# Two token mixers of an encoder trunk on one Trainium2 core: weight remainders moved from GpSimd to VectorE, output sums merged, and the order of TensorE's work around the scan groups and the attention rows changed

## The chip, the core and the metric

The kernel runs on one core of one Trainium2 chip. A core has TensorE (matmuls into PSUM banks), VectorE, ScalarE, GpSimd and SyncE, the last of which here only issues DMAs. The profile calls them PE (with PEld for TensorE's loads of stationary operands), DVE, ACT, POOL and SP. The metric is the time of one execution in microseconds on the device.

## The reference

512 tokens of width 1024 in float32 go through two layers. Each layer adds a mixer and a gated FFN to the residual stream:

```python
def even_mixer(x, ...):                        # layer 0
    proj = rms_norm(x, mix_norm) @ w_in        # q, k, v | z, xbc, dt
    na_out = neighbourhood_attention(q, k, v, na_rel_bias)      # 8 heads of 64
    xbc = silu(centred_depthwise_conv(xbc, conv_w, conv_b))     # xs, bm, cm
    y = ssd_scan(forward) + flip(ssd_scan(backward)) + D_skip * xs   # 16 heads, 4 groups, chunks of 128
    ssd_out = gated_group_rms_norm(y, z, out_norm)              # norm over a group's 256 columns
    return concatenate([na_out, ssd_out]) @ w_out
def odd_mixer(x, ...):                         # layer 1
    q, k, v = split(rms_norm(x, mix_norm) @ w_qkv)              # 16 query heads, 4 key/value heads of 64
    q, k = apply_rope(rms_norm(q)), apply_rope(rms_norm(k))
    return softmax(q @ k.T * scale) @ v @ w_out
def swiglu_ffn(x, norm_g, w13, w2):            # after each mixer
    g, u = split(rms_norm(x, norm_g) @ w13)
    return (silu(g) * u) @ w2
```

## The kernel before

Activations lie with the channels on the 128 partitions and the 512 tokens along the free axis. The residual stream is eight tiles of 128x512, `res[0..7]`. A float32 product is made of three matmuls: each operand is split into a high half (a rounded copy, made by ScalarE, names ending in `h`) and a low half (the remainder, one subtraction, names ending in `l`), and `mm3` adds low by high, high by low and high by high in one PSUM bank. The `w_l`, `wq_l`, `wo_l` of the profile are such remainders of weights, made in `load_w`: SyncE loads a raw block, ScalarE copies it, and the engine given as `eng` subtracts.

TensorE's filler work is a generator. `stream(blocks, ahead)` goes through weight blocks and yields after each `mm3` (three matmuls, called a step here), and `run(n)` does n steps. What lies between the steps is the work with dependent chains.

`even_mixer` records TensorE's order by hand in its second half (the other engines' order is found by the Tile scheduler). There are four scan groups g. The projections of group g are steps 64+48g to 64+48(g+1); the last step of its fourth channel block triggers one Silu over 128x3072 (L545). `LEAD[g]` steps later, `ssd_group` begins with the transposes `bt` (L563), `xt` and the products `cb`, then, with `SSD_QUOTA[g]` steps between its phases, the states `st`, the first `yd`/`yo` (L651, L664) and the second. `NORM_LAG[g]` steps after the group's end come the row sums `gs` (L688) for its normalisation, whose results `so_xh`, `so_xl` are operands of the output products. Those products are the last filler: `oA` for each of 8 output tiles, over 8 of the 10 operand blocks, and after every three tiles a "rest" with the two blocks of the third group (weights `wq{0,3,6}`). The last group's two blocks are done at the end, in `tail`.

`odd_mixer` is ordered by the Tile scheduler on all engines. Filler work is the q projections of query groups 1 to 3 and then the output products (`out_blocks`), whose operands `ctxb` come out of the attention. In iteration i, `scores(i)` makes two score tiles `os`, maximum (L1276, VectorE), exponential (ScalarE), reciprocal, and a rescaling on GpSimd (L1280); transposes follow two and values three iterations later. `quota[i]` steps of filler are spread over iteration i. A finished q projection triggers the rotation and norm of the group (`q_finish`), whose remainders `qa_sl`, `qb_sl` are made on GpSimd, like `cx_sl` of finished heads. The remainders of the value weights (`wgvl`, L1349) and of all filler weights (`wq_l`, `wo_l`) are also GpSimd's. The output products come in three parts of two operand blocks, each part once over all 8 output tiles with one addition to `res` for each tile (L1328); the fourth part is in `tail`.

In the FFNs the order of TensorE, VectorE and ScalarE is written out. The last lines add each of the final products to `res` and store it (L994, L996).

## Time and profile before

| | |
|---|---|
| time, median of 3 runs | 1282.05 us (1279.4 to 1282.43) |
| profiled execution, its own time | 1281.94 us |
| its span, first to last instruction | 1280.2 us |
| TensorE busy | 1258.6 us, 98% of the span |
| VectorE, ScalarE, GpSimd busy | 990.8, 723.9, 154.4 us |
| mean granted TensorE clock | 0.996 of full speed |

The span lacks what lies before the first and after the last instruction, 1.74 us here. A busy engine has an instruction running; TensorE's matmuls overlap, so 128x512 matmuls that last 0.39 us each follow one another every 0.227 us. The granted clock is given as a share of full speed.

### The profile page before, as it was taken

The page shows a single profiled execution, that of the slowest core. Times are in us where ns is not written, and L with a number is a line of the kernel's source. Part 1 is how long each engine was busy: PE and PEld are TensorE (multiplying, and loading weights), DVE is VectorE, ACT ScalarE, POOL GpSimd, SP SyncE. Part 2 cuts the span into 40 slices and gives each one's busy share as a digit, 9 for nine tenths or more (in the row PEclk, how much of TensorE's full clock was granted, in tenths as well). Part 3 has the DMA queues.
Part 4 walks back from the last instruction along what each step waited for, and adds up shares of the span by engine and source line. Part 5 has one row for each costly group of instructions (what it writes and reads, how often), then busy time and mean ns, then how long its engine had stood idle before and what let it go on. Part 6 is the DMA issues. An engine that isn't in the chain of part 4 may idle for free.

```text
span 1280.2 us, 19995 instructions
## 1 busy us (share of the span) xinstructions
PE 1258.6 (98%) x7502; PEld 1100.6 (86%) x7502; DVE 990.8 (77%) x1649; ACT 723.9 (57%) x1367; POOL 154.4 (12%) x177
## 2 busy tenths in 40 slices
PE   9999999999999999999999999999999999999998
PEld 8778788777888899989998878778888999889987
DVE  6788798898689888739953778998889988549732
ACT  6676578778365455515633548867564556325521
POOL 5022111011000000000000325655100000000000
PEclk9999999999999999999999999999999999999999
DMA  6335443546332333323223352321223333323132
GB/s 232 103 108 158 111 141 116 165 128 193 108 132 83 107 108 114 118 82 100 77 79 109 132 116 83 83 67 34 86 80 99 115 102 114 115 82 100 55 118 93
DMA packets 52081, 139.03 MB, mean 109 GB/s; under 512 B 6992, under 2 KB 8144, under 8 KB 51984
## 3 DMA queue, kind: packets, MB, share of 16 engines
q1 hardware_dynamic: 51696, 137.23, 35.0%
q8 instruction: 59, 0.97, 0.3%
q10 hardware_dynamic: 288, 0.52, 0.1%
q14 instruction: 38, 0.31, 0.1%
HBM read 127.11 MB, written 2.23 MB: 101 GB/s over the span
## 4 chain that ended last, share of the span: by engine, by line
PE 71%; DVE 14%; ACT 7%; issue 4%; DMA 2%; POOL 0%; SPq 0%; DVEq 0%; ACTq 0%; POOLq 0%
PE fo L160 5%; PE fo L161 5%; PE fo L162 5%; PE fa L162 5%; PE fa L161 5%; PE fa L160 5%; PE fb L162 3%; PE fb L161 3%; PE fb L160 3%; PE opt L1289 2%; PE g L160 2%; PE g L161 2%; PE g L162 2%; PE vps L281 2%; PE fc L162 1%
## 5 line engine op out<-in xcount | busy, mean ns | idle before, releaser
L147 ACT ACTIVATE wf_h<-wf_r 128x1024 fp32r<-128x1024 f32 (+1 forms) x76 | 69.5, 919 | 125.9 <-PE fo L162 68.0
L160 PE MATMUL fo<-hh,wf_l 128*128 128x512 f32 x352 | 137.2, 390 | 0.4 <-DVE wf_l L149 0.4
L161 PE MATMUL fo<-hl,wf_h 128*128 128x512 f32 x352 | 137.0, 389 | 0.0
L162 PE MATMUL fo<-hh,wf_h 128*128 128x512 f32 x352 | 136.9, 389 | 0.0
L994 DVE TENSOR_TENSOR xr<-xr,fo 128x512 f32<-128x512 f32 x48 | 32.2, 685 | 111.3 <-PE fo L162 111.3
L149 DVE TENSOR_TENSOR wf_l<-wf_r,wf_h 128x1024 fp32r<-128x1024 f32 (+1 forms) x76 | 78.8, 1054 | 15.5 <-ACT wf_h L147 15.5
L160 PEld LDWEIGHTS fo<-hh,wf_l 128*128 128x128 f32 x352 | 66.1, 188 | 14.7 <-DVE wf_l L149 1.2
L162 PEld LDWEIGHTS fo<-hh,wf_h 128*128 128x128 f32 x352 | 66.1, 188 | 13.9
L161 PEld LDWEIGHTS fo<-hl,wf_h 128*128 128x128 f32 x352 | 66.1, 188 | 13.5
L160 PE MATMUL g<-n_xh,w_l 128*128 128x512 f32 x192 | 76.8, 400 | 0.0
L161 PE MATMUL g<-n_xl,w_h 128*128 128x512 f32 x192 | 75.1, 391 | 0.5 <-DVE n_xl L184 0.5
L162 PE MATMUL g<-n_xh,w_h 128*128 128x512 f32 x192 | 75.3, 392 | 0.0
L920 ACT ACTIVATE sl<-sb 128x256 f32<-128x256 f32 x34 | 14.2, 419 | 90.7 <-DVE sb L919 90.7
L1349 POOL TENSOR_TENSOR wgvl<-wgv_r,wgvh 128x512 fp32r<-128x512 f32 x4 | 6.5, 1635 | 402.2 <-ACT wgvh L1348 400.3
L1280 POOL TENSOR_SCALAR op<-op,osum 128x512 f32<-128x512 f32 x64 | 45.7, 723 | 54.0 <-DVE osum L1279 36.1
L1278 ACT ACTIVATE op<-os,omx 128x512 f32<-128x512 f32 x64 | 43.5, 685 | 13.6 <-DVE omx L1276 12.2
L1292 ACT ACTIVATE opt<-opt 128x512 fp32r<-128x512 f32 x64 | 38.1, 598 | 20.4 <-PE opt L1289 20.1
L1293 DVE TENSOR_TENSOR opt<-opt,opt 128x512 fp32r<-128x512 f32 x64 | 43.6, 684 | 5.6 <-ACT opt L1292 4.7
L801 ACT ACTIVATE sa<-fa 128x256 f32<-128x256 f32 x68 | 25.4, 374 | 36.9 <-PE fa L162 36.9
L1276 DVE TENSOR_REDUCE omx<-os 128x1 f32<-128x512 f32 x64 | 42.0, 681 | 5.2 <-PE os L1274 5.1
L801 ACT ACTIVATE gh<-gr 128x1024 fp32r<-128x1024 f32 x34 | 35.6, 1047 | 13.7 <-PE fo L162 8.8
L161 PEld LDWEIGHTS g<-n_xl,w_h 128*128 128x128 f32 x192 | 36.1, 188 | 7.4 <-DVE n_xl L184 0.8
(2635 smaller groups left out, 4354.0 us busy)
## 6 DMA issues: line engine op xcount, KB each, us to landing
ur<-in_w_fa SPq DMA_DIRECT2D x34, 512.0 KB, 3.5
gr<-in_w_fa SPq DMA_DIRECT2D x34, 512.0 KB, 3.6
w_r<-in_w_ssd SPq DMA_DIRECT2D x24, 512.0 KB, 3.6
wf_r<-in_w_fa SPq DMA_DIRECT2D x20, 512.0 KB, 3.6
wf_r<-in_w_fb SPq DMA_DIRECT2D x32, 320.0 KB, 3.0
wf_r<-in_w_fb SPq DMA_DIRECT2D x16, 512.0 KB, 3.6
wo_r<-in_w_o SPq DMA_DIRECT2D x14, 512.0 KB, 3.8
nb<-in_nab SPq DMA_DIRECT2D x16, 256.0 KB, 3.2
```

The lines of the kernel that those rows point to most:

```text
L147: A.activation(hi[:, 0:cols], raw, AF.Copy)
L149: (eng or V).tensor_tensor(lo[:, 0:cols], raw, f(hi)[:, 0:cols], ALU.subtract)
L160: T.matmul(ps, wl[:, a], xh[:, b], start=first, stop=False, skip_group_check=skip)
L161: T.matmul(ps, wh[:, a], xl[:, b], start=False, stop=False, skip_group_check=skip)
L162: T.matmul(ps, wh[:, a], xh[:, b], start=False, stop=last, skip_group_check=skip)
L801: A.activation(dst, src, AF.Copy, scale=scale)
L994: V.tensor_tensor(res[o], res[o], self.banks[o], ALU.add)
L1276: V.tensor_reduce(mx, sps, AX.X, ALU.max, negate=True)
L1278: A.activation(p_, sps, AF.Exp, bias=mx, accum_out=sums)
L1280: G.tensor_scalar(p_, p_, sums, 1.0, ALU.mult, ALU.mult)
L1292: A.activation(hl[:, 0:S], pt, AF.Copy)
L1293: V.tensor_tensor(hl[:, S:2 * S], pt, f(hl[:, 0:S]), ALU.subtract)
```

## The change

1. `vec`, the small table of gains, is loaded by ScalarE's DMA queue instead of SyncE's, ahead of everything.
2. In `even_mixer`, `LEAD`, `SSD_QUOTA` and `NORM_LAG` get other numbers. The largest: the last group begins 12 steps after its projections instead of 0, its row sums come 12 instead of 14 steps after it, the third group's row sums 10 instead of 6 steps after that group, and between the third group's two output halves no step is left.
3. In `odd_mixer`, 16 remainders of weights (six `wq_l` and six `wo_l` of 128x1024, four `wgvl` of 128x512) go from GpSimd to VectorE. The remainders of activations and the rescaling stay on GpSimd.
4. The output products of parts 0 and 1 are summed in one bank: 12 matmuls a bank, two output tiles from a weight block, one addition where there were two (8 additions fewer). They begin when both parts' operands are there. Part 2 stays as it was.
5. The quota of iterations 9, 14, 18, 21 and 25 becomes 8, 0, 5, 9 and 4, where it was 2, 2, 2, 3 and 2 (all others are equal or differ by one).
6. The last output tile of the second FFN is added and stored in two halves.

The number of matmuls is the same.

```diff
-LEAD = (12, 12, 12, 0)
-SSD_QUOTA = ((10, 8, 10, 2, 12), (10, 8, 10, 2, 12), (10, 8, 10, 2, 12), (10, 8, 10, 2, 12))
-NORM_LAG = (12, 12, 6, 14)
+OD_FILL = 8
+OD_AFTER = 4
+OD_QUOTA = (5, 5, 4, 2, 2, 2, 2, 2, 2, 8, 2, 2, 2, 2, 0, 2, 3, 2, 5, 2, 2, 9, 2, 2, 2, 4, 3, 2, 2, 3, 2, 2, 3, 3, 3)
+LEAD = (15, 12, 14, 12)
+SSD_QUOTA = ((10, 9, 10, 2, 12), (10, 8, 10, 2, 12), (10, 8, 10, 0, 12), (10, 8, 10, 2, 12))
+NORM_LAG = (12, 12, 10, 12)
...
+        nc.scalar.dma_start(vect, vec)
         A.preload_act_table_set(LNEXP)
...
-        nc.sync.dma_start(vect, vec)
...
                 if k == self.hi - 1:
-                    V.tensor_tensor(res[o], res[o], self.banks[o], ALU.add)
-                    if self.final and layer == 1:
-                        nc.sync.dma_start(out[o], res[o])
+                    last = self.final and layer == 1
+                    for at in (LOH, HIH) if last and o == KB - 1 else (ALL,):
+                        V.tensor_tensor(res[o][:, at], res[o][:, at], self.banks[o][:, at], ALU.add)
+                        if last:
+                            nc.sync.dma_start(out[o][:, at], res[o][:, at])
...
-        def out_blocks(part):
-            def matmuls(w, half):
-                while ctxb[2 * part + 1] is None:
+        def out_blocks(parts):
+            per = 8 // (2 * len(parts))
+
+            def matmuls(w, t):
+                while ctxb[2 * parts[-1] + 1] is None:
                     yield
-                for o in range(4 * half, 4 * half + 4):
-                    ps = bank(f"o1{part}_{o}")
-                    for k in range(2):
-                        mm3(ps, w, (o % 4 * 2 + k) * P, ctxb[2 * part + k], ALL, k == 0, k == 1)
-                        yield
+                for n in range(per):
+                    o = per * t + n
+                    ps = bank(f"o1{parts[0]}_{o}")
+                    for m, part in enumerate(parts):
+                        for k in range(2):
+                            mm3(ps, w, ((m * per + n) * 2 + k) * P, ctxb[2 * part + k], ALL, m + k == 0,
+                                k == 1 and part == parts[-1])
+                            yield
                     V.tensor_tensor(res[o], res[o], ps, ALU.add)
...
+            def load(t):
+                half, at = divmod(t * per, 4)
+                return load_w([w_o1[part, half][:, 2 * P * at:2 * P * (at + per)] for part in parts], 1024,
+                              f"wo{parts[0]}_{t}", V)
...
-            G.tensor_tensor(lo, part, f(hi), ALU.subtract)
+            V.tensor_tensor(lo, part, f(hi), ALU.subtract)
...
-        blocks = (list(q_blocks(1, G)) + list(q_blocks(2, G)) + list(q_blocks(3, G))
-                  + [b for part in range(3) for b in out_blocks(part)])
+        blocks = (list(q_blocks(1, V)) + list(q_blocks(2, V)) + list(q_blocks(3, V))
+                  + [b for parts in ((0, 1), (2,)) for b in out_blocks(parts)])
...
-            n = quota[i]
+            n = OD_QUOTA[i]
```

Three places in the order show what moves. The first is TensorE at the end of the third scan group (number 2: `yo` is its last product) and the start of the last one (`bt` reads `grp`, the Silu's result). Before:

```order
L664 MATMUL yo_1_0_2992<-grp_392,H_2698 128x128 x3
L664 MATMUL yo_1_1_3001<-grp_392,H_2698 128x128 x3
L563 MATMUL bt_3020<-cstt,grp_393 128x128 x4
L570 MATMUL xt_0_3027<-cstt,grp_393 128x128 x4
L570 MATMUL xt_1_3034<-cstt,grp_393 128x128 x4
L576 MATMUL cb_3041<-grp_393 128x128 x4
L160 MATMUL oA_2963<-so_0_xh,wo_l 128x512
```

Now:

```order
L667 MATMUL yo_1_0_2992<-grp_392,H_2704 128x128 x3
L667 MATMUL yo_1_1_3001<-grp_392,H_2704 128x128 x3
L163 MATMUL oA_2963<-so_0_xh,wo_l 128x512
L164 MATMUL oA_2963<-so_0_xl,wo_h 128x512
L165 MATMUL oA_2963<-so_0_xh,wo_h 128x512
...
L163 MATMUL oA_3032<-nch_1663,wo_l 128x512
L164 MATMUL oA_3032<-ncl_1664,wo_h 128x512
L165 MATMUL oA_3032<-nch_1663,wo_h 128x512
L566 MATMUL bt_3045<-cstt,grp_393 128x128 x4
L573 MATMUL xt_0_3052<-cstt,grp_393 128x128 x4
```

Eighteen `oA` matmuls of 512 columns stand between `yo` and `bt` where none stood. Behind them the third group's row sums `gs` come 36 `oA` and `st` matmuls ahead of the first "rest" (the first use of that group's normalised blocks), where they came 48 ahead; the 12 that are gone are `oA`.

The second place is VectorE in the second half of scan group 1. `cf` is an operand of TensorE's `yd` (L651), `grp` a convolution (L528), `w_5_l` the remainder of a weight block. Before:

```order
L646 TENSOR_TENSOR cf_2444<-cf_2444,m_2443 128x512
L644 TENSOR_TENSOR cf_2466<-cf_2466,cb_2467 128x512
L528 SCALAR_TENSOR_TENSOR grp_392<-g_3_2435,vect,grp_392 128x510
L149 TENSOR_TENSOR w_5_l<-w_5_r,w_5_h 128x1024
L646 TENSOR_TENSOR cf_2466<-cf_2466,m_2465 128x512
L528 SCALAR_TENSOR_TENSOR grp_392<-g_3_2435,vect,grp_392 128x511
L149 TENSOR_TENSOR w_0_l<-w_0_r,w_0_h 128x1024
```

Now:

```order
L649 TENSOR_TENSOR cf_2444<-cf_2444,m_2443 128x512
L531 SCALAR_TENSOR_TENSOR grp_392<-g_3_2435,vect,grp_392 128x510
L649 TENSOR_TENSOR cf_2466<-cf_2466,m_2465 128x512
L531 SCALAR_TENSOR_TENSOR grp_392<-g_3_2435,vect,grp_392 128x511
L152 TENSOR_TENSOR w_5_l<-w_5_r,w_5_h 128x1024
```

Both `cf` products come ahead of the remainder `w_5_l`.

The third place is VectorE in the attention of `odd_mixer` around iterations 9 and 10: `omx` and `osum` belong to score tiles, `q_ra`, `q_rb` and `oq_m` to the rotation and norm of a query group, `opt` to transposed probabilities. Before:

```order
L1276 TENSOR_REDUCE omx<-os_2_8313 128x1
L1276 TENSOR_REDUCE omx<-os_3_8323 128x1
L1315 TENSOR_TENSOR ocx_8301<-oc_8221,oct_8302 64x512
L1152 TENSOR_TENSOR q_rb_8337<-q_1_8055,qt_tab 128x512
L1293 TENSOR_TENSOR opt_1_8310<-opt_1_8305,opt_1_8310 128x512
L1279 RECIPROCAL osum<-osum 128x1
L1153 TENSOR_TENSOR q_ra_8336<-q_ra_8336,q_rb_8337 128x512
L1279 RECIPROCAL osum<-osum 128x1
L1151 TENSOR_TENSOR q_ra_8341<-q_0_7870,qt_tab 128x512
L1152 TENSOR_TENSOR q_rb_8342<-q_1_8055,qt_tab 128x512
L1195 SCALAR_TENSOR_TENSOR oq_m<-oq_ss,oem 128x512
L1153 TENSOR_TENSOR q_ra_8341<-q_ra_8341,q_rb_8342 128x512
```

Now:

```order
L1281 TENSOR_REDUCE omx<-os_2_8314 128x1
L152 TENSOR_TENSOR wq_1_l<-wq_1_r,wq_1_h 128x1024
L1284 RECIPROCAL osum<-osum 128x1
L1281 TENSOR_REDUCE omx<-os_3_8324 128x1
L152 TENSOR_TENSOR wo_0_l<-wo_0_r,wo_0_h 128x1024
L1284 RECIPROCAL osum<-osum 128x1
L1158 TENSOR_TENSOR q_ra_8337<-q_ra_8337,q_rb_8338 128x512
L1157 TENSOR_TENSOR q_rb_8343<-q_1_8055,qt_tab 128x512
L1200 SCALAR_TENSOR_TENSOR oq_m<-oq_ss,oem 128x512
L1158 TENSOR_TENSOR q_ra_8342<-q_ra_8342,q_rb_8343 128x512
L1298 TENSOR_TENSOR opt_0_8404<-opt_0_8399,opt_0_8404 128x512
L152 TENSOR_TENSOR wo_1_l<-wo_1_r,wo_1_h 128x1024
```

Three remainders of 128x1024 stand between the small operations; the rotation's first products have moved ahead of these rows. Between score tiles 13 and 22, two more such remainders come, and three additions to `res` (L1328) stand where six stood; two products of a rotation leave that stretch to earlier rows.

A fourth move needs no rows. On ScalarE, in front of the attention, the copy `wq1_1_h` stood between the logarithm and the exponential of the key norm `ok_r`; now it stands behind that norm's three operations. On VectorE the sum `oqsq`, which TensorE's first head-norm product waits for, now has `wq_1_l`, two of the four `wgvl` and both `kab` remainders ahead of it on that norm's chain, where only one `kab` was.

## Rows read from the trace of the kernel before

**Rows 1.** The page's busy engines, and its group of GpSimd's rescaling.

```profile
PE 1258.6 (98%) x7502; PEld 1100.6 (86%) x7502; DVE 990.8 (77%) x1649; ACT 723.9 (57%) x1367; POOL 154.4 (12%) x177
...
L1280 POOL TENSOR_SCALAR op<-op,osum 128x512 f32<-128x512 f32 x64 | 45.7, 723 | 54.0 <-DVE osum L1279 36.1
```

**Rows 2.** Waits of PE by line and releaser: us in total, times, longest.

```profile
PE os L1273 <- ACT op L1278: 2.7, 1, 2.7
PE oq_ss L1193 <- DVE oqsq L1243: 2.4, 1, 2.4
...
PE os L1273 <- DVE oq_m L1195: 1.4, 1, 1.4
```

**Rows 3.** Windows: length, busy PE, PEld, DVE, ACT, POOL; PEclk, DMA share, GB/s.

```profile
289.90:293.60 3.70, 3.63 (x21) 3.63 (x21) 1.87 (x5) 3.44 (x6) 0.00 (x0) 0.60 0.92 247
...
741.00:744.00 3.00, 3.00 (x12) 2.02 (x11) 3.00 (x4) 0.79 (x3) 2.36 (x1) 0.59 0.72 158
...
804.80:808.50 3.70, 3.67 (x24) 3.25 (x24) 3.70 (x7) 2.98 (x6) 0.00 (x0) 1.00 0.12 48
...
795.99:862.40 66.41, 61.44 (x352) 50.08 (x350) 60.46 (x113) 50.13 (x106) 40.23 (x38) 0.97 0.26 72
862.40:918.80 56.40, 56.40 (x342) 48.97 (x342) 49.11 (x96) 38.73 (x82) 23.56 (x27) 1.00 0.17 57
817.90:830.05 12.15, 11.23 (x73) 9.40 (x72) 10.16 (x21) 9.81 (x23) 7.34 (x11) 1.00 0.41 109
830.05:849.00 18.95, 16.50 (x95) 13.52 (x93) 18.81 (x32) 13.66 (x27) 11.65 (x10) 1.00 0.17 58
```

**Rows 4.** Timeline of the first microseconds: start, duration, engine, instruction, [idle before <-releaser].

```profile
0.73 0.39 SPq L240 DMA_DIRECT2D vect<-in_vec  x1
1.18 0.42 SPq L249 DMA_DIRECT2D x<-in_xt  x1
```

**Rows 5.** Timeline, end of scan group 2 to the third "oA" behind it.

```profile
287.15 2.76 ACT L545 ACTIVATE grp<-grp 128x3072 f32<-128x3072 f32 x1
...
289.97 1.11 PE L563 MATMUL bt<-cstt,grp 128*128 128x128 f32 x4 [3.96 <-ACT grp L545]
...
298.19 0.39 PE L160 MATMUL oA<-so_xh,wo_l 128*128 128x512 f32 x1
...
299.78 0.39 PE L161 MATMUL oA<-so_xl,wo_h 128*128 128x512 f32 x1
```

**Rows 6.** Timeline around the first "rest" of the output products.

```profile
307.82 0.74 DVE L184 SCALAR_TENSOR_TENSOR so_xl<-yn,vect,so_xh 128x512 fp32r<-128x512 f32 x1
...
309.95 0.39 PE L161 MATMUL oA<-so_xl,wq_h 128*128 128x512 f32 x1
```

**Rows 7.** Timeline in the second half of scan group 1.

```profile
237.53 1.21 DVE L149 TENSOR_TENSOR w_l<-w_r,w_h 128x1024 fp32r<-128x1024 f32 x1
...
239.40 1.09 PE L651 MATMUL yd<-cf,xtok 128*64 128x128 f32 x14 [0.83 <-DVE cf L646]
```

**Rows 8.** Timeline from the key norm to the first head-norm product of odd_mixer.

```profile
727.72 2.27 DVE L218 TENSOR_TENSOR ortt<-ort 128x4 f32<-128x4 f32 x1 [1.24 <-ACT ort L217]
730.02 0.16 DVE L203 SCALAR_TENSOR_TENSOR ortt<-ortt,ortm 128x4 f32<-128x4 f32 x1
...
732.34 1.04 ACT L147 ACTIVATE wq_h<-wq_r 128x1024 fp32r<-128x1024 f32 x1
...
734.60 1.81 DVE L203 SCALAR_TENSOR_TENSOR ok_t<-ok_t,ok_m 128x512 f32<-128x512 f32 x1 [2.10 <-ACT ok_t L211]
...
740.31 0.68 DVE L1204 TENSOR_TENSOR kab<-k_ra,kab 128x512 fp32r<-128x512 f32 x1
```

**Rows 9.** VectorE's groups from 756 to 919: busy, mean ns | idle before.

```profile
L1255 DVE TENSOR_TENSOR q_ra<-q_ra,oq_r 128x512 f32<-128x512 f32 x6 | 5.9, 1020 | 0.0
L1153 DVE TENSOR_TENSOR q_ra<-q_ra,q_rb 128x512 f32<-128x512 f32 x6 | 5.8, 963 | 0.0
...
L149 DVE TENSOR_TENSOR wt_l<-wt_r,wt_h 128x1024 fp32r<-128x1024 f32 x2 | 2.4, 1221 | 0.3 <-ACT wt_h L147 0.3
```

More of the change, by code (lines that the diff above doesn't have):

```diff
@@ L1243, in matmuls @@
                     V.tensor_tensor(sqs[0], sqs[0], sqs[1], ALU.add)
-                    after(4, lambda: q_finish(g, banks, sqs[0]))
+                    after(OD_AFTER, lambda: q_finish(g, banks, sqs[0]))
             sqs = []
@@ L1317, in values @@
                 ctxb[h // 2] = split(cx, f"cx{h}", xgslot if h >= 12 else ctxslot, V if h >= 14 else G)
-        def out_blocks(part):
-            def matmuls(w, half):
-                while ctxb[2 * part + 1] is None:
+        def out_blocks(parts):
+            per = 8 // (2 * len(parts))
+            def matmuls(w, t):
+                while ctxb[2 * parts[-1] + 1] is None:
                     yield
-                for o in range(4 * half, 4 * half + 4):
-                    ps = bank(f"o1{part}_{o}")
-                    for k in range(2):
-                        mm3(ps, w, (o % 4 * 2 + k) * P, ctxb[2 * part + k], ALL, k == 0, k == 1)
-                        yield
-                    V.tensor_tensor(res[o], res[o], ps, ALU.add)
-            for half in range(2):
-                yield (lambda half=half: load_w(w_o1[part, half], 1024, f"wo{part}_{half}", G)), \
-                    (lambda w, half=half: matmuls(w, half))
+                for n in range(per):
[6 more added lines that the diff above has]
+                            yield
+                    V.tensor_tensor(res[o], res[o], ps, ALU.add)
+            def load(t):
+                half, at = divmod(t * per, 4)
+                return load_w([w_o1[part, half][:, 2 * P * at:2 * P * (at + per)] for part in parts], 1024,
+                              f"wo{parts[0]}_{t}", V)
+            for t in range(8 // per):
+                yield (lambda t=t: load(t)), (lambda w, t=t: matmuls(w, t))
         def run(gen, n=None):
@@ L1369, in odd_mixer @@
             step(True)
-        blocks = (list(q_blocks(1, G)) + list(q_blocks(2, G)) + list(q_blocks(3, G))
-                  + [b for part in range(3) for b in out_blocks(part)])
+        blocks = (list(q_blocks(1, V)) + list(q_blocks(2, V)) + list(q_blocks(3, V))
+                  + [b for parts in ((0, 1), (2,)) for b in out_blocks(parts)])
         fill = stream(blocks, 2)
-        run(fill, 8)
+        run(fill, OD_FILL)
         step(True)
@@ L1376, in odd_mixer @@
             stack_k(j)
-        quota = (5, 5, 4) + 13 * (2,) + (3, 2, 2, 2, 2, 3, 2, 2, 2, 2, 3, 2, 2, 3, 2, 2, 3, 3, 3)
         lag_t, lag_v = 2, 3
         for i in range(32 + lag_v):
-            n = quota[i]
+            n = OD_QUOTA[i]
             cuts = (0, (n + 2) // 3, (2 * n + 2) // 3, n)
```

## The prediction

> **What bounds the kernel now.** I read the page's busy engines first. TensorE is busy 1258.6 us of the span of 1280.2 [rows 1], so at most 21.6 us of waits are to be had, plus what a lower clock costs. The change leaves the number of matmuls alone; it can gain only there, or lose by new waits. Next I read TensorE's waits by line and releaser [rows 2], looked each up in the timeline for its place, and then cut the stretches around them into windows [rows 3], where the granted clock and VectorE's load stand side by side. Four waits lie where the change works: 3.96 us for the Silu of the last scan group [rows 5], 2.4 for `oqsq` ahead of the attention, 2.7 for a probability tile inside it [rows 2], 0.83 for `cf` in scan group 1 [rows 7]. Two drag the clock down: behind the first it is 0.60 over 3.70 us, behind the second 0.59 over 3.00 [rows 3], about the lower of its two levels, 1.2 of 2.4 GHz. A wait of 1.4 us at the start of an attention row [rows 2] left it at 1.00 over the 3.70 us that followed [rows 3]. The FFNs aren't touched except for the last tile.
>
> **The start.** SyncE issues `vect` at 0.73 and the first `x` at 1.18 [rows 4]. With `vect` on ScalarE's queue, `x` can go 0.45 earlier, and all waits for it. The bounds are -0.45 and 0 (0 if the table is then the later of the two). I take -0.45.
>
> **The last scan group.** `bt` waits 3.96 us; the Silu ends at 287.15 + 2.76 = 289.91, `bt` begins at 289.97, so TensorE was ready at 286.01 [rows 5]. Now 18 `oA` matmuls stand there. One comes every (299.78 - 298.19) / 7 = 0.227 us [rows 5], so they last 4.09 and end just behind the Silu: -3.96. They aren't new work; they are missing later. The clock of 0.60 behind the wait cost 3.70 x 0.40 = 1.48 [rows 3]; with no wait it goes: -1.48, at worst 0.
>
> What is missing later is cover. The third group's second normalised block is finished at 307.82 + 0.74 = 308.56, and its use comes at 309.95 [rows 6]. Twelve `oA` fewer between that group's row sums and the use are 2.72 us: the use would come at 307.23, 1.3 us too early: +1.3 (0 if the normalisation comes earlier too, 2.7 if all of the cover is lost). The last group's own row sums stand twelve `oA` nearer to their use in the closing products; no wait is listed there now, so I put +0.3 between 0 and the same 2.7. The other LEAD and quota numbers move products past products and stand at 0, hidden under filler at full rate.
>
> **Scan group 1.** The 1.21 us of `w_5_l` stood ahead of the second `cf` on VectorE; TensorE waited 0.83 for it [rows 7]. With both `cf` ahead, -0.83; at worst 0, if the ScalarE step before it is what counts. Even mixer together: -3.96 - 1.48 - 0.83 + 1.3 + 0.3 = -4.7.
>
> **Ahead of the attention.** The sum `oqsq` hangs on the key norm's chain. A 128x4 product there took 2.27 us where its neighbour of that size took 0.16 [rows 8]; GpSimd ran weight remainders beside it. ScalarE's `wq_h`, 1.04, stood in the chain and now stands behind; `ok_t` took 1.81 [rows 8] where the same kind of operation takes 0.74 [rows 6]. That is 2.1 + 1.0 + 1.1 = 4.2 back. Against it stand what VectorE now has ahead of `oqsq`: two `wgvl` at 0.68 and a second `kab` at 0.68 [rows 8], one `wq_l` at 1.21 [rows 7], 3.3 in all. The wait falls by 0.9 to about 1.5, nearest to the wait that left the clock alone, so its cost, 3.00 x 0.41 = 1.23 [rows 3], goes too: -2.1. The bounds are 0 (VectorE's queue eats all) and -3.6 (wait and clock loss gone).
>
> **The attention, rows 9 to 22.** From 795.99 to 862.40 VectorE is busy 60.46 of 66.41 and idle 5.95; TensorE is busy 61.44, partly at a lower clock (0.97 on the mean), and stands 4.97. In its middle, from 830.05 to 849.00, VectorE is busy 18.81 of 18.95 while TensorE is at 16.50 [rows 3]. So VectorE sets this stretch. It gets five remainders at 1.22 (`wt_l`, which is VectorE's already [rows 9]), +6.1. It loses three additions at 0.68, -2.0, and two products of a rotation to earlier rows, -1.4. And GpSimd's remainders no longer lengthen its two-input operations: q_ra took 1.020 and 0.963 on the mean of six each [rows 9] against 0.68 undisturbed [rows 8], 3.7 us over the twelve; GpSimd keeps `qa_sl`, `qb_sl`, `cx_sl`, so I give back 2.5. Together +0.2: 60.7. What is left is how much of the idle 5.95 closes. Since the middle has 0.14 of it only, the idle time lies around the rows outside, where eight steps of filler now stand in row 9 instead of two. I let 1.6 close: 60.7 + 4.3 = 65.0, -1.4. That is a choice, about a quarter of the idle. The bounds are -5.6 (nearly all closes) and +3.8: a GpSimd rescaling lasts 0.723 [rows 1], and if each of five remainders had to wait out one, 3.6 come on top of 0.2 with the idle as it is.
>
> The rows show a 128x4 operation held for 2.27 us beside GpSimd's remainder [rows 8]. The Trainium skill, page "SBUF — State Buffer", section "Who interferes with whom", has the rule for it: VectorE and GpSimd share a pair of ports under an exclusive lock, and a VectorE operation with two SBUF inputs contends with a GpSimd operation that reads SBUF. It speaks against the change as well: a remainder has two SBUF inputs, and GpSimd's rescaling still reads. By that rule the five remainders could wait 3.6 us in all, which makes 1276.9 of the sum below. The trace half agrees: `wt_l`, in the attention's window, took 1.221 [rows 9], and `w_l` far from it 1.21 [rows 7].
>
> **After row 22** TensorE is busy 56.40 of 56.40 [rows 3], with one step more of filler than before: 0. VectorE has 49.11 of work there [rows 3], and loses five additions. Merging the sums saves TensorE nothing; where the merged banks wait for their last operand, the scheduler has other products. The last tile's halves: two additions, at least half of 0.68 each, then half the bytes to store: 0, within 0.3 either way.
>
> **The sum.** -0.45 - 4.7 - 2.1 - 1.4 = -8.6 against the profiled execution's 1281.94: 1273.3. The median of the runs lies 0.11 above that execution, which changes nothing.
>
> **The rivals.**
> *All covers hold and VectorE's idle time closes.* Start -0.45, last scan group and `cf` -6.27 with nothing new, `oqsq` -3.6, attention -5.6: 1266.0. For it: the waits end each on one thing that is moved away. Against it: the normalised block has 1.39 us to spare now and loses 2.72 [rows 6].
> *The wait for the Silu moves along.* The 18 `oA` delay nothing that the Silu needs, but VectorE and ScalarE queues are rearranged, and if `grp` ends four microseconds later, `bt` waits as before with its clock: 1273.3 + 5.4 = 1278.7. Against it: the last projection step stands where it stood.
> *VectorE fills up.* The remainders collide with the rescaling (+3.8 in place of -1.4), and nothing comes back ahead of the attention (0 in place of -2.1): 1273.3 + 5.2 + 2.1 = 1280.6.
> *Slower: the clock falls in the thin rows 14 to 22.* While the merged products wait for heads 6 and 7, the rows run with few fillers and TensorE pauses often. Between 817.90 and 849.00 it has 11.23 + 16.50 = 27.7 us of work [rows 3]; at half clock that is 55.5, where the stretch lasts 31.1, +24.4: 1297.7. It decides from about half of it on, +12.4, which passes 1285.8. Against it: from 817.90 to 830.05, with 0.92 us of pauses, the clock is 1.00, and so it is from 830.05 to 849.00 with 2.45 [rows 3].
> The Trainium skill, page "TensorE: Matmul & The Clock Gate", section "A second HAM failure mode: psum-queue depth-cycling", describes such micro-idles between groups of matmuls that make the clock swing; the trace shows none of it in these windows.
>
> **How the numbers follow.** The forecast gets 0.55 (with its own range of 1269.5 to 1277.5), the covers that all hold 0.13, the Silu's wait that moves along 0.13, VectorE that fills up 0.14, the falling clock 0.05. Faster or slower is counted from 0.3%, 3.8 us, about what a measurement can tell here, so from 1278.1 and 1285.8. Faster: the first two, 0.68, and 0.10 of the third and fourth, whose times lie a little above 1278.1. Slower: the last and 0.01 of the fourth, 0.06. The same: the other 0.16. The range takes in the third case, most of the fourth's side and the upper part of the second: 1267.5 to 1280.0.
>
> **What would show it.** Right: no wait of `bt` over 0.3 us and a clock of 1.00 behind it; a wait of about 1.3 at the first "rest"; `cf` gone from the waits; `oq_ss` waiting about 1.5 with the clock at 1.00; rows 9 to 22 about 65 us. Wrong, if the clock falls anywhere it was full, if five remainders last well over 1.22, or if the merged products keep TensorE waiting for `cx` behind row 16.

## The result and the profile after

The changed kernel takes 1269.29 us (median of 4 runs, 1268.36 to 1269.74) where the kernel before took 1281.06 on the same chip (4 runs, 1279.4 to 1282.43). The ratio is 0.9908 with a 95% interval of 0.9891 to 0.9925, some 11.8 us less. Run again with three experiments it came to 0.9908 (0.9895 to 0.9922). The prediction was 1273.3, 1267.5 to 1280.0: inside its range, with the gain taken for 8.6.

The profiled execution took 1269.74 us with a span of 1267.9. On the page, the lines that answer to [rows 1]:

```profile
PE 1254.8 (99%) x7502; PEld 1096.8 (87%) x7502; DVE 990.5 (78%) x1658; ACT 723.5 (57%) x1367; POOL 120.4 (9%) x161
...
L1285 POOL TENSOR_SCALAR op<-op,osum 128x512 f32<-128x512 f32 x64 | 48.1, 758 | 507.0 <-DMA QS<-qa_sh 435.1
```

TensorE stands 13.1 us of the span instead of 21.6. GpSimd has lost 34.0 us of work, and VectorE, which got all of the remainders, has not gained any: 990.5 after 990.8. Besides the 8.5 us of waits, TensorE's busy time is 3.8 us less with the same 7502 matmuls; the stretches of low clock in which matmuls took longer are gone, as the windows below show. TensorE's waits, the list that answers to [rows 2]:

```profile
PE kss L365 <- ACT ksq L363: 1.4, 1, 1.4
PE gs L691 <- ACT xtok L575: 1.3, 2, 0.8
...
PE oA L164 <- DVE so_xl L187: 0.9, 1, 0.9
PE opt L1294 <- DVE opt L1298: 0.7, 1, 0.7
PE oq_ss L1198 <- ACT op L1283: 0.5, 1, 0.5
...
PE os L1278 <- ACT op L1283: 0.5, 2, 0.3
PE vps L284 <- ACT wv_h L269: 0.4, 1, 0.4
PE nsc L405 <- DMA kl<-kl: 0.4, 1, 0.4
```

The waits for the Silu at `bt`, for `cf`, for `oqsq` and the 2.7 us for a probability tile are gone from the list. What is new is 0.9 at the first "rest" (`oA` for `so_xl`), which the prediction had at 1.3, and 1.3 at the row sums `gs`, which it did not have. In the attention small waits (0.7 for `opt`, 0.5 at `oq_ss`, 0.5 at `os` and 0.4 for `cx_sh`) stand where 2.7, 1.4, 0.6 and 0.3 stood. (`oq_ss` in this list is a later group's.) The windows that answer to [rows 3] are those behind `bt`, behind the first `oq_ss`, of rows 9 to 22, and from row 22 to the closing products:

```profile
288.00:291.70 3.70, 3.70 (x28) 3.44 (x28) 2.31 (x6) 3.69 (x6) 0.00 (x0) 1.00 0.82 228
...
732.52:735.52 3.00, 3.00 (x20) 2.52 (x21) 3.00 (x5) 0.56 (x2) 0.00 (x0) 1.00 1.00 257
...
786.88:850.28 63.40, 61.15 (x351) 49.62 (x349) 58.71 (x115) 50.74 (x107) 28.58 (x35) 1.00 0.25 67
850.28:906.58 56.30, 56.30 (x343) 49.23 (x342) 48.30 (x90) 37.40 (x78) 21.20 (x24) 1.00 0.17 57
```

In all four the granted clock is 1.00, where three of their counterparts had 0.60, 0.59 and 0.97. Rows 9 to 22 take 63.40 instead of 66.41, the rows behind them 56.30 instead of 56.40.

To see where the time came from I took the starts of the same TensorE instruction in both traces: the first product for the time steps (`dps`, at 124.16 before), the first projection of the attention mixer (`kpa`, 710.59), the first score of row 1 (`os`, 761.25), and the span's end (1280.15). The changed kernel is ahead of the kernel before by 1.66 at `dps`, 5.93 at `kpa`, 9.55 at row 1 and 12.23 at the end. So 1.66 came at the start, 4.27 in the scan groups, 3.62 ahead of the attention and 2.68 in and behind it; the scan groups' share takes in the FFN behind them. The experiments are read with the same cuts below, because a stretch shows smaller differences than the whole time. They have a limit: each is one execution against one, and in stretches where nothing was changed the table below still has differences of up to 0.5 us.

### The profile page after: what moved, and what is told of

It reads as the page before. It is cut to its first block, busy times and chain, and to the rows that moved or that the text cites. A ratio compares the mean times of both kernels' runs of the same rounds, so it can differ in the third digit from the quotient of the medians.

```text
span 1267.9 us, 19987 instructions
## 1 busy us (share of the span) xinstructions
PE 1254.8 (99%) x7502; PEld 1096.8 (87%) x7502; DVE 990.5 (78%) x1658; ACT 723.5 (57%) x1367; POOL 120.4 (9%) x161
## 4 chain that ended last, share of the span: by engine, by line
PE 80%; DVE 10%; ACT 6%; issue 3%; DMA 1%; ACTq 0%; DVEq 0%
PE fo L163 5%; PE fo L165 5%; PE fo L164 5%; PE fa L165 5%; PE fa L164 5%; PE fa L163 5%; PE g L164 3%; PE g L163 3%; PE g L165 3%; PE fb L165 3%; PE fb L164 3%; PE fb L163 3%; PE opt L1294 2%; PE vps L284 2%; PE fc L165 1%
## 5 line engine op out<-in xcount | busy, mean ns | idle before, releaser
L999 DVE TENSOR_TENSOR xr<-xr,fo 128x512 f32<-128x512 f32 (+1 forms) x49 | 32.3, 674 | 112.1 <-PE fo L165 112.1
L165 PEld LDWEIGHTS g<-n_xh,w_h 128*128 128x128 f32 x192 | 36.0, 188 | 7.4
```

What stands on the lines that cost most here:

```text
L165: T.matmul(ps, wh[:, a], xh[:, b], start=False, stop=last, skip_group_check=skip)
L999: V.tensor_tensor(res[o][:, at], res[o][:, at], self.banks[o][:, at], ALU.add)
```

## The experiments

All times are ratios to the kernel before on the same chip, which took 1279.95, 1280.31 and 1280.57 us (medians) in the three sets, and 1281.06 beside the first row.

| kernel | median, us | ratio (95% interval) | to `dps` | scan groups | ahead of row 1 | row 1 to end |
|---|---|---|---|---|---|---|
| the changed kernel | 1269.29 | 0.9908 (0.9891-0.9925) | -1.66 | -4.27 | -3.62 | -2.68 |
| 12 the same again | 1268.54 | 0.9908 (0.9895-0.9922) | -1.92 | -4.76 | -3.77 | -2.69 |
| 1 table's load alone | 1280.66 | 1.0005 (0.9996-1.0015) | -1.56 | +0.26 | +0.22 | -0.05 |
| 2 even mixer's numbers alone | 1275.90 | 0.9965 (0.9951-0.9979) | -1.06 | -4.86 | +0.20 | -0.12 |
| 3 attention's part alone | 1274.53 | 0.9959 (0.9944-0.9974) | -1.39 | +0.49 | -3.49 | -2.78 |
| 4 remainders alone | 1276.04 | 0.9967 (0.9954-0.9980) | -1.12 | +0.42 | -3.76 | -1.30 |
| 5 changed, remainders back | 1272.67 | 0.9942 (0.9927-0.9957) | -1.40 | -4.80 | -0.32 | -3.14 |
| 6 changed, old quota | 1271.29 | 0.9933 (0.9918-0.9948) | -0.57 | -4.20 | -3.78 | -0.77 |
| 7 changed, sums apart | 1272.81 | 0.9942 (0.9925-0.9958) | -0.91 | -4.72 | -3.92 | +0.30 |
| 8 last group's LEAD alone | 1281.93 | 1.0009 (0.9999-1.0018) | -1.04 | +1.67 | +0.17 | -0.09 |
| 9 changed, GpSimd rescales only | 1273.11 | 0.9944 (0.9931-0.9958) | -1.78 | -4.79 | -3.76 | +1.49 |
| 10 changed, remainders of the attention back | 1269.65 | 0.9916 (0.9902-0.9930) | -1.16 | -4.29 | -3.00 | -3.20 |
| 11 as 10, row sums later | 1271.31 | 0.9930 (0.9917-0.9944) | -1.62 | -3.52 | -3.25 | -3.29 |

The four columns on the right are differences in us between the profiled execution of that kernel and the one of before, for each stretch (the scan groups' column runs from `dps` to `kpa`).

The column "to `dps`" has a trap in it. All thirteen other executions are 0.6 to 1.9 us ahead there, those with nothing changed in that stretch too (2, 3, 4 and 8). The one profiled execution of before was slow there: its `nsc` waited 1.40 for the landing of `kl`, and in no other execution is that wait over 0.52. So that column says nothing on the change, and about 1 us of the 12.23 belongs to that one execution. The three columns to its right don't hang on it.

**1. The table's load alone** (on the kernel before):

```diff
+        nc.scalar.dma_start(vect, vec)
         A.preload_act_table_set(LNEXP)
...
-        nc.sync.dma_start(vect, vec)
```

> Only the load of the gain table is moved to ScalarE's queue. In the changed kernel TensorE is 0.55 us ahead at the first row-sum product and 1.66 us ahead from the neighbourhood scores on, because the wait of `nsc` for `kl` fell from 1.40 to 0.41. Theory A, the table's load is worth all of it: `nsc` waits about 0.4 here too, and the span falls by 1.6 us. Theory B, the load is worth its issue alone and the landing of `kl` differs from one execution to the next: the first row-sum product comes 0.5 earlier, `nsc` waits anything between 0.4 and 1.4, and the time falls by 0.5 us, which the runs can't tell from none.

Measured 1.0005: no gain. The first row-sum product comes 0.06 us later than before. In the changed kernel's timeline, which answers to [rows 4]:

```profile
0.74 0.40 ACTq L237 DMA_DIRECT2D vect<-in_vec  x1
0.74 0.38 SPq L252 DMA_DIRECT2D x<-in_xt  x1
...
4.25 0.23 ACT L497 ACTIVATE ea<-vect 128x32 f32<-128x32 f32 x1 [1.80 <-DMA vect<-in_vec]
4.38 0.71 ACT L186 ACTIVATE early<-x,vect 128x512 fp32r<-128x512 f32 x1
```

`x` is issued 0.45 earlier, as the sum had it. But the table, issued beside it and not ahead of it, is now there at 4.25 where its first reader ran at 2.78 before, and the first use of both, `early`, begins at 4.38 where it began at 3.85. The term's other bound was the true one: the table is now the later of the two, and the wait only changed its name.

**2. The even mixer's numbers alone**, **3. the attention mixer's part alone**:

```diff
-LEAD = (12, 12, 12, 0)
-SSD_QUOTA = ((10, 8, 10, 2, 12), (10, 8, 10, 2, 12), (10, 8, 10, 2, 12), (10, 8, 10, 2, 12))
-NORM_LAG = (12, 12, 6, 14)
+LEAD = (15, 12, 14, 12)
+SSD_QUOTA = ((10, 9, 10, 2, 12), (10, 8, 10, 2, 12), (10, 8, 10, 0, 12), (10, 8, 10, 2, 12))
+NORM_LAG = (12, 12, 10, 12)
```

Experiment 3 is the changed kernel with these three lines, the table's load and the last tile's halves put back.

> Only LEAD, SSD_QUOTA and NORM_LAG as in the change. By the sum's steps the waits for the Silu (3.96) and `cf` (0.83) and 1.48 of lower clock go, and new waits come at the first `rest` (0.9 as in the changed kernel) and at two row sums (1.3): 4.1 us less, 1277, with everything behind the even mixer as before (`oq_ss` waits 2.4, clock 0.59 behind it). Rival, the even mixer's part in the changed kernel hangs on the earlier start: under 3 us less, the Silu's wait in part still there.

> Only the attention mixer's part of the change: remainders on VectorE, merged sums, uneven quota. If the parts add up, it is worth what the changed kernel's trace shows from the first FFN's end on: about 6 us less, 1275, `oq_ss` waiting under 0.3 with the clock at 1.00, rows 9 to 22 about 63.4 us. Rival, the parts overlap (what the even mixer gains is in part given back here, or the other way round): this part and the even mixer's add up to over 1.5 us more or less than the whole change's 11.8.

Measured 0.9965 and 0.9959. Each part moves its own stretches and leaves the others within 0.5: -4.86 in the scan groups for the one, -3.49 and -2.78 around the attention for the other. In the traces the parts add: -4.86 - 6.27 = -11.1 against -10.6 in the same three columns of the changed kernel. By the times it isn't decided: 0.35% and 0.41% make 0.76%, the whole 0.92%. That is 2 us short, more than the 1.5 that the expectation had named as the sign of its rival, but each of the three has an interval of 0.14 to 0.17% either way. The last tile's halves are in the whole alone and show nothing: from the start of the last matmul to the span's end it is 4.12 us with them, and without them 4.24 in the kernel before and 4.13 in experiment 3.

**4. The remainders alone** (quota and three output parts as before):

```diff
-            G.tensor_tensor(lo, part, f(hi), ALU.subtract)
+            V.tensor_tensor(lo, part, f(hi), ALU.subtract)
-                yield (lambda half=half: load_w(w_o1[part, half], 1024, f"wo{part}_{half}", G)), \
+                yield (lambda half=half: load_w(w_o1[part, half], 1024, f"wo{part}_{half}", V)), \
-        blocks = (list(q_blocks(1, G)) + list(q_blocks(2, G)) + list(q_blocks(3, G))
+        blocks = (list(q_blocks(1, V)) + list(q_blocks(2, V)) + list(q_blocks(3, V))
```

> Only the sixteen remainders go from GpSimd to VectorE; the quota and the three separate output parts stay. Theory A, the port that VectorE shares with GpSimd's remainders was the cost: VectorE's two-input operations fall back to about 0.70 us (`q_ra` took 0.96 and 1.02), the wait of `oq_ss` and its clock loss go, and most of the attention mixer's gain comes, 4 us or more, 1277 or less. Theory B, VectorE fills up without the merged sums (eight additions more, 5.4 us) and the even quota: `oq_ss` gains its 2.5 us, but rows 9 to 22 take as long as before or longer, 1279 or more.

Measured 0.9967, 4.2 us less by the ratio, as theory A had it. The clock behind `oq_ss` is full and `q_ra` of L1255 is at 0.840 instead of 1.020. This is the larger share of the attention part by itself, but not all of it and not where I had it: -3.76 ahead of row 1, -1.30 behind.

**5. The changed kernel with all sixteen remainders back on GpSimd**, the complement:

```diff
-            V.tensor_tensor(lo, part, f(hi), ALU.subtract)
+            G.tensor_tensor(lo, part, f(hi), ALU.subtract)
-                              f"wo{parts[0]}_{t}", V)
+                              f"wo{parts[0]}_{t}", G)
-        blocks = (list(q_blocks(1, V)) + list(q_blocks(2, V)) + list(q_blocks(3, V))
+        blocks = (list(q_blocks(1, G)) + list(q_blocks(2, G)) + list(q_blocks(3, G))
```

> The changed kernel with its sixteen remainders back on GpSimd (merged sums, uneven quota, even mixer as changed). The remainders alone, moved to VectorE in the kernel before, gave 5.0 us from the first projection of the attention mixer to its closing products. Theory A, they carry that gain whatever the quota: 4.5 to 6 us slower than the changed kernel, `oq_ss` waiting 2 us or more with a clock near 0.6 behind it, `q_ra` back near 1.0 us. Theory B, merged sums and quota would have found most of it by themselves: under 3 us slower.

Measured 0.9942, 4.4 us slower than the changed kernel by the ratios and 2.8 by the stretches of the attention part. Neither theory had it: the whole gain ahead of row 1 is gone (-0.32), and the gain behind it is all there (-3.14, and -2.68 with them on VectorE, which is within the scatter). In the stretch ahead of the attention the old picture is back. Its wait, and the timeline that answers to [rows 8]:

```profile
PE oq_ss L1198 <- DVE oqsq L1248: 2.2, 1, 2.2
...
PE gv L1372 <- DVE oq_m L1200: 0.7, 1, 0.7
```

```profile
721.37 2.38 POOL L152 TENSOR_TENSOR wq_l<-wq_r,wq_h 128x1024 fp32r<-128x1024 f32 x1
721.46 2.32 DVE L206 SCALAR_TENSOR_TENSOR ortt<-ortt,ortm 128x4 f32<-128x4 f32 x1
...
725.93 1.04 ACT L150 ACTIVATE wq_h<-wq_r 128x1024 fp32r<-128x1024 f32 x1
...
727.05 2.40 POOL L152 TENSOR_TENSOR wq_l<-wq_r,wq_h 128x1024 fp32r<-128x1024 f32 x1 [3.30 <-ACT wq_h L150]
...
728.19 1.81 DVE L206 SCALAR_TENSOR_TENSOR ok_t<-ok_t,ok_m 128x512 f32<-128x512 f32 x1 [2.10 <-ACT ok_t L214]
```

The changed kernel in the same place:

```profile
721.43 0.16 DVE L221 TENSOR_TENSOR ortt<-ort 128x4 f32<-128x4 f32 x1 [1.25 <-ACT ort L220]
...
722.12 0.16 DVE L206 SCALAR_TENSOR_TENSOR ortt<-ortt,ortm 128x4 f32<-128x4 f32 x1
...
726.24 0.69 DVE L206 SCALAR_TENSOR_TENSOR ok_t<-ok_t,ok_m 128x512 f32<-128x512 f32 x1 [0.17 <-ACT ok_t L214]
...
731.78 0.68 DVE L1248 TENSOR_TENSOR oqsq<-oqsq,oqsq 128x512 f32<-128x512 f32 x1
```

The same two operations that took 2.32 and 1.81 beside GpSimd's remainders take 0.16 and 0.69 without them, and each of the long ones ends just behind the remainder beside it (723.78 after 723.75, 730.00 after 729.45). ScalarE's `wq_h` is back in the chain too. One thing more is to be seen in experiment 5: its wait of 2.2 us left the clock at 1.00, where that of 2.4 before was followed by 0.59 [rows 3]. The clock that it kept did not become time: `gv` waits 0.7 us for `oq_m` behind it, which is not in the list of the kernel before, and the whole stretch is only 0.32 shorter.

```profile
734.04:737.04 3.00, 3.00 (x19) 2.31 (x20) 3.00 (x4) 1.35 (x3) 2.36 (x1) 1.00 0.59 127
```

**6. The changed kernel with the quota of before**, **7. with its output parts apart again**:

```diff
-OD_QUOTA = (5, 5, 4, 2, 2, 2, 2, 2, 2, 8, 2, 2, 2, 2, 0, 2, 3, 2, 5, 2, 2, 9, 2, 2, 2, 4, 3, 2, 2, 3, 2, 2, 3, 3, 3)
+OD_QUOTA = (5, 5, 4) + 13 * (2,) + (3, 2, 2, 2, 2, 3, 2, 2, 2, 2, 3, 2, 2, 3, 2, 2, 3, 3, 3)
```

```diff
-                  + [b for parts in ((0, 1), (2,)) for b in out_blocks(parts)])
+                  + [b for parts in ((0,), (1,), (2,)) for b in out_blocks(parts)])
```

> The changed kernel with the quota of before. The whole attention part was 1.2 us better than the remainders alone, so quota and merged sums together are worth about that. If the quota is what makes the merged sums go, 1 to 3 us slower than the changed kernel, with waits of TensorE for `cx` or `os` between rows 16 and 22; if it is worth nothing, within 1 us.

> The changed kernel with the first two output parts apart again (eight additions more on VectorE, 5.4 us, but fillers from head 4 on). If VectorE's load sets rows 9 to 22, up to 2 us slower, as three of the additions lie there; if the earlier fillers make up for it, no slower, and the waits between rows 16 and 19 (0.74 for `opt`, 0.38 for `cx`) go.

Measured 0.9933 and 0.9942. From row 1 to the end, each of the two edits is worth the gain only with the other: merged sums with the old quota -0.77, the new quota with separate sums +0.30, both -2.68 (neither, in experiment 4, -1.30). In 6 the merged products wait where the forecast had seen a danger (0.9 for `cx_sl`). In 7 the fillers go ahead faster, and then the closing products stand for the last heads:

```profile
PE t L163 <- ACT cx_sh L1167: 1.4, 1, 1.4
```

The expectation that the waits between rows 16 and 19 would go with the sums apart failed: `os` waits 1.5 there. And 3.0 us slower is more than either of its branches had.

**8. The last group's LEAD alone** (on the kernel before):

```diff
-LEAD = (12, 12, 12, 0)
+LEAD = (12, 12, 12, 12)
```

> The kernel before with the last group alone begun twelve steps later (LEAD's last number 12). By the sum's steps: the Silu's wait (3.96) and the clock behind it (1.48) go, `cf` stays at 0.7 to 0.8, no new wait at the third group's row sums if they now come ahead of the banks that `xt` takes; 5 us less in the even mixer. Rival: the wait is not for the Silu but moves with the start of the group, over 2 us left at `bt`.

Measured 1.0009: none of the 5 us that I expected. `bt` waits no more, and the third group's row sums wait in its stead, longer than `bt` did. Wait, clock behind it, and ScalarE's timeline:

```profile
PE gs L688 <- DVE gs_ql L685: 4.8, 1, 4.8
```

```profile
294.19:298.00 3.81, 3.81 (x18) 3.51 (x18) 0.00 (x0) 2.45 (x4) 0.00 (x0) 0.56 0.88 243
```

```profile
285.12 1.28 ACT L545 ACT_TABLE_LOAD   x1 [1.60 <-DVE grp L528]
286.42 2.78 ACT L545 ACTIVATE grp<-grp 128x3072 f32<-128x3072 f32 x1
289.20 1.28 ACT L548 ACT_TABLE_LOAD   x1
290.49 1.15 ACT L681 ACTIVATE gsq<-y 128x512 f32<-128x512 f32 x2
...
292.80 0.61 ACT L684 ACTIVATE gs_qh<-gsq 128x512 fp32r<-128x512 f32 x1
```

This is the step of which the prediction had the half. Two things of TensorE's hang on ScalarE's Silu: `bt`, which reads its result, and `gs`, whose squares stand behind it in ScalarE's queue, with two table loads around it. In the old order `gs` came after `bt`'s wait and never showed. With `bt` moved and NORM_LAG left at 6, `gs` comes first, finds its operand not made, and TensorE stands 4.80 us with the clock at 0.56 behind it. In the changed kernel, with NORM_LAG at 10, `gs` comes behind `bt`, `xt`, `cb` and twelve `oA`, and its operand is ready ahead of it; what it still waits for is `xtok`:

```profile
292.22 0.69 DVE L688 TENSOR_TENSOR gs_ql<-gsq,gs_qh 128x512 fp32r<-128x512 f32 x1
...
293.69 0.50 PE L691 MATMUL gs<-gs_ql,ones_r 128*128 128x512 f32 x1 [0.51 <-ACT xtok L575]
```

So I read the change of NORM_LAG from 6 to 10, which I had costed by the cover that it takes from the "rest", as what lets the gain of LEAD through. That is argued from the order and these rows: no run changes LEAD and NORM_LAG alone, and experiment 2, which has the gain, changes SSD_QUOTA and two other LEAD numbers with them.

**9. GpSimd left with the rescaling alone** (on the changed kernel):

```diff
-            eng = G if g else V
+            eng = V
-                ctxb[h // 2] = split(cx, f"cx{h}", xgslot if h >= 12 else ctxslot, V if h >= 14 else G)
+                ctxb[h // 2] = split(cx, f"cx{h}", xgslot if h >= 12 else ctxslot, V)
```

> The changed kernel with the remainders of activations (`qa_sl`, `qb_sl`, `cx_sl`) on VectorE too, so that GpSimd has nothing but the rescaling in the attention: 13 operations of 0.68 us, 8.8 us, come onto VectorE. If the time follows VectorE's load in rows 9 to 22, where some seven of them fall, 3 us or more slower than the changed kernel. If the shared port is what counts, VectorE's other operations get shorter again and it is no slower.

Measured 0.9944, 4.2 us slower from row 1 to the end. VectorE's other operations didn't get shorter (`q_ra` 0.733 and 0.676 after 0.731 and 0.678): there was nothing left to win from GpSimd's side, and the load is what counts here.

**10. Only the remainders that are needed ahead of the attention on VectorE**, **11. the same with the second group's row sums later**, **12. the changed kernel again**:

```diff
-        blocks = (list(q_blocks(1, V)) + list(q_blocks(2, V)) + list(q_blocks(3, V))
+        blocks = (list(q_blocks(1, V)) + list(q_blocks(2, G)) + list(q_blocks(3, G))
-                              f"wo{parts[0]}_{t}", V)
+                              f"wo{parts[0]}_{t}", G)
```

Experiment 11 has these and one number more:

```diff
-NORM_LAG = (12, 12, 10, 12)
+NORM_LAG = (12, 14, 10, 12)
```

> The changed kernel with only those remainders on VectorE that are needed ahead of the attention (four `wgvl`, two `wq_l` of group 1); the ten others are back on GpSimd. Measured so far: the remainders' gain lies ahead of row 1 (3.3 to 3.7 us), and behind it merged sums and quota with the remainders on GpSimd gained 3.1, with them on VectorE 2.7. Theory A, the gain is local: 3.6 us ahead of row 1 and 3.1 behind it, 0.4 us better than the changed kernel. Theory B, GpSimd's remainders hold VectorE in rows 9 to 22 as they did before: 1 us or more slower than the changed kernel.

> As the kernel before this one, with the second group's row sums two steps later (NORM_LAG 14), so that they come behind the evacuation of `xt`, for which TensorE waited 0.77 us. If the bank is all they wait for: 0.7 us less in the even mixer. Rival: the group's normalised blocks come later by 1.4 us, and nothing waits for them yet, so no loss; a loss would show as a wait at the first `oA`.

> The changed kernel again, to be compared with the three others on one chip: 0.990 to 0.992 of the kernel before, `nsc` waiting about 0.4.

Measured 0.9916, 0.9930 and 0.9908. The ten remainders inside the attention can lie on either engine: -3.20 behind row 1 with GpSimd, -2.68 and -2.69 with VectorE, and -3.00 against -3.62 and -3.77 ahead of it, so neither the sum nor the time is better. That is so although GpSimd then holds VectorE as it did before; the group of this kernel that answers to [rows 9]:

```profile
L1158 DVE TENSOR_TENSOR q_ra<-q_ra,q_rb 128x512 f32<-128x512 f32 x6 | 7.3, 1219 | 0.0
```

Theory B of experiment 10 falls with that row: the operation is held more than before (0.963), and nothing waits for it. Experiment 11 lost 0.8 us in the scan groups against experiment 10: the wait at that `gs` went (0.8), in line with the bank as what it waited for, and a wait of 1.8 for `cf` came up behind it. No version here beats the changed kernel.

```profile
PE yd L654 <- DVE cf L649: 1.8, 1, 1.8
```

## Why the forecast was right, and what in it was not

The direction, the places and the range held. By its own steps, against the changed kernel's stretches:

| step | forecast | measured |
|---|---|---|
| start | -0.45 | 0 (experiment 1; the trace's -1.66 belongs to the execution of before) |
| last scan group and `cf` | -4.7 | -4.3 to -4.9 |
| ahead of the attention | -2.1 | -3.5 to -3.9 |
| the attention | -1.4 | -2.7 (rows 9 to 22 alone -3.0) |
| sum | -8.6 | 10.6 to 11.2 less in the three stretches; 11.8 by the medians |

**The start** came out at the other of its two bounds; the table became the later load.

**The last scan group** came out as forecast, in part by luck. The waits of 3.96 and 0.83 went, the clock stands at 1.00 where it was 0.60, and the new wait at the "rest" is 0.9 for 1.3 (0.4 in other executions of the same order). The closing products have no wait: the +0.3 was not needed. In its place came 1.3 at two `gs`, which now wait for ScalarE's evacuation of `xt`; in the kernel the second `xt` and `gs` take their banks from the same pair. And the reason that LEAD works at all was missing: experiment 8 shows that the forecast's rival "the wait for the Silu moves along" is what happens, by another way than I had given it, unless the row sums move too.

**Ahead of the attention** the mechanism was right: GpSimd's remainders held VectorE on the key norm's chain, and experiments 4 and 5 give the gain with them alone and take it away with them alone. What they don't separate is VectorE's two held operations from ScalarE's `wq_h`, which leaves the chain and comes back in the same runs. The size was off. I let the wait of `oq_ss` fall by 0.9 to 1.5; it fell to 0.14 (TensorE is busy 6.24 of the 6.38 us from 729.12 on). The products that came into the chain were counted at their full length, 3.3 us, though VectorE stood 2.10 us in that chain before [rows 8], where a `wq_l` now lies, and the timeline shows 128x512 operations starting every 0.60. What went of that wait (2.2) and the low clock behind it (1.23) make up nearly the whole 3.62; with both gone the prediction's bound was -3.6. By the starts 1.1 of it seem to lie between rows 0 and 1, but there only five filler matmuls are missing, which now stand ahead of row 0. The windows from the first score of row 0 to that of row 1, before and now:

```profile
756.95:761.25 4.30, 4.30 (x20) 3.57 (x19) 1.62 (x4) 2.88 (x6) 2.48 (x2) 1.00 0.46 105
```

```profile
748.53:751.70 3.17, 3.17 (x15) 2.63 (x14) 2.52 (x5) 2.17 (x5) 0.00 (x0) 1.00 0.45 103
```

How much of the 3.62 is the clock's stays open: experiment 5 had the clock at 1.00 and gained 0.32.

The Trainium skill's rule of the shared ports (page "SBUF — State Buffer", section "Who interferes with whom") is borne out there, 2.32 against 0.16 and 1.81 against 0.69. What I drew from it against the change, 3.6 us for five remainders beside the rescaling, did not come: `wo_l` takes 1.222 in the attention of the changed kernel (1.296 at most, in experiment 7). GpSimd's rescaling is at 0.758 after 0.723, and no wait of TensorE for it is in the list.

```profile
L152 DVE TENSOR_TENSOR wo_l<-wo_r,wo_h 128x1024 fp32r<-128x1024 f32 x6 | 7.3, 1222 | 0.1
L1260 DVE TENSOR_TENSOR q_ra<-q_ra,oq_r 128x512 f32<-128x512 f32 x6 | 4.2, 731 | 0.0
L1158 DVE TENSOR_TENSOR q_ra<-q_ra,q_rb 128x512 f32<-128x512 f32 x6 | 4.1, 678 | 0.0
```

**The attention** was the weakest step. The share of idle time that I had chosen was near: of VectorE's 5.95 us of idle in rows 9 to 22, 1.26 closed (63.40 - 58.71 = 4.69 are left), for the 1.6 forecast. The term that failed is VectorE's busy time: 60.46 with +0.2 was to become 60.7 and became 58.71. The operations were added up at their full lengths; by those there is indeed as much work as before (66.7 us for 66.4), but VectorE's operations overlap, by 5.9 us before and 8.0 now, and busy time counts an overlap once. The prediction also passed over a third low clock in the kernel before, though it had the 0.97 of the whole stretch. It named two, but behind the 2.7 us wait of `os` at row 19 the clock is 0.51 over 3.00 us, 1.47 us by its own way of counting:

```profile
849.21:852.21 3.00, 3.00 (x9) 2.40 (x10) 2.94 (x7) 1.15 (x4) 2.22 (x3) 0.51 0.41 92
```

A slip in its rival of the falling clock changes nothing: 1273.3 + 12.4 is 1285.7, just short of the 1285.8 that it was to pass.

The step would have rested better on VectorE's load over the whole attention. From row 1 to the second FFN's row sums TensorE has the same matmuls in every kernel; the windows give VectorE's busy time and the length:

| kernel | VectorE busy, us | length, us |
|---|---|---|
| new quota, merged, remainders on GpSimd (5) | 154.1 | 179.3 |
| the same, with the six remainders ahead of row 1 on VectorE (10) | 155.0 | 179.2 |
| the changed kernel | 159.1 | 179.7 |
| new quota, sums apart (7) | 163.6 | 182.8 |
| new quota, merged, GpSimd rescales only (9) | 167.0 | 183.9 |
| old quota, merged (6) | 160.5 | 181.7 |
| old quota, sums apart, remainders on VectorE (4) | 164.8 | 181.1 |
| the kernel before | 159.3 | 182.3 |

With the new quota the length follows VectorE's load: 5 us more cost 0.4, 9.5 us more cost 3.5, 12.9 cost 4.6. I read this as an edge: up to about 159 us VectorE's work hides, and beyond it half or more shows. That is argued from the order of five kernels, not shown: they differ in more than the load (1.4 of the 3.1 us that experiment 7 loses is the wait of the closing products for `cx_sh`, behind fillers that ran out earlier), and no run changes the load alone. If it holds, the changed kernel sits at that edge: its eight remainders there (9.7 us at full length) are paid by the merged sums (5.4 us) and by operations that GpSimd no longer holds (`q_ra` alone 7.3 + 3.9 in experiment 10 against 8.3). That would be why merged sums look like nothing on TensorE, and why taking them out costs 3. The rival "VectorE fills up" did not come at this load, and experiments 7 and 9, with 4 to 8 us more, are what it would look like; "the clock falls in the thin rows" did not occur, the clock is 1.00 in every one of these kernels' windows from row 1 on, but for the kernel before.

With the old quota the table has no such order (164.8 goes with 181.1, 159.3 with 182.3). One event sets the kernel before apart, the 2.7 us wait at row 19 and the low clock behind it. Each of the edits shrinks it by itself: remainders alone leave 1.25 us of that wait, merged sums and quota none (0.3 at row 18), and in both the clock stays at 1.00. That is a likely reason why -1.30 and -3.14 don't add to -2.68. What exactly the new quota does in rows 9 to 21 that is worth 2 us (6 against the changed kernel) I have not settled; there is no run that changes one of its numbers alone.

## What to carry to other kernels

When a wait on a busy engine is covered by later work, list all of the waiting engine's instructions that hang on that same queue: the next one takes the wait over, as the row sums did when LEAD moved alone, and an order that works has moved both. Count an engine's work by the starts of its operations and not by their lengths, where they overlap: both of the sums here that added lengths came out too dear. An engine's load in a stretch may have an edge, below which more work is free; then an edit that frees such an engine looks worthless on the critical engine's count, and pays for another edit that loads it. Here that is a reading, and a run that changes the load alone would test it. And compare a profiled execution with more than one other before reading a stretch: 1 us of the difference between the traces here was one slow DMA landing in the trace of before.

## What the runs showed of the hardware that I had not expected

A VectorE operation on 128x4 elements was held for 2.1 to 2.2 us while GpSimd made a 128x1024 remainder, and runs in 0.16 without it. The other way round the loss is small: 64 rescalings on GpSimd went from 0.723 to 0.758 us with sixteen remainders moved to VectorE (0.786 in experiment 4). The clock was at 1.00 behind a wait of 2.2 us (experiment 5) and at 0.59, 0.51, 0.60 and 0.56 behind waits of 2.4, 2.7, 4.0 and 4.8. The small table, issued at 0.74 us beside the first large load, was read at 4.25; issued at 0.73 with the large loads 0.45 us behind it, it was read at 2.78.
